# Inverse and decays of a delta rule, and two scalings of a state space, moved to GpSimd in a planned layer kernel

## The chip, the cores and the metric

The kernel runs on one core of a Trainium2 chip. The metric is device time in microseconds (us), the median of several executions; smaller is better. The engines are TensorE (PE in the rows, its weight loads PEld), VectorE (DVE), ScalarE (ACT), GpSimd (POOL) and the DMA queue of SyncE (SP).

## The reference

One layer of a hybrid mixer in float32: 1024 tokens and 256 context tokens, model width 2048. After a modulated RMS norm and one wide projection `u @ w_in`, half of the width goes through a state space (16 heads of 64, state 128) and half through a gated delta rule (8 heads of 128), both in both directions and in chunks of 128 tokens; then gating, norms, the output projection and a residual. What the change touches:

```python
# delta rule, per head, direction and chunk
decay = exp(where(incl, gcum[..., :, None] - gcum[..., None, :], -inf))
a_strict = where(strict, einsum('bhcik,bhcjk->bhcij', k_beta, k) * decay, 0.0)
sol = triangular_solve(a_strict, rhs, lower=True, unit_diagonal=True)
attn = einsum('bhcik,bhcjk->bhcij', q, k) * decay
# state space, per group and direction
lmat = exp(where(causal, seg, -inf))                      # seg: difference of cumulated decays
y_diag = einsum('bcgrqs,bcsgrp->bcqgrp', cb * lmat, xdt)  # xdt = x * dt
states = einsum('bcsgn,bcsgrp->bcgrpn', bm, xdt * decay_end)
```

## The kernel before, in words

The projection runs in blocks of 128 output channels. A block's weights come as two raw tiles, are split into a high and a low half in float16 (`split`: squares and first half on ScalarE, L410 and L413, second half on VectorE, L415), and three products per block of 128 inputs are summed on TensorE (`products`, L439), 512 tokens at a time into PSUM banks `ps_d` and `ps_e`. `conv_block` empties a bank: one ScalarE instruction (L492, L494), four VectorE instructions for the other taps (L500), a tanh (L504) and a product (L505). The taps are scaled by one small GpSimd instruction per block (L485).

The eight heads of the delta rule follow one another as a pipeline, written in `steps` of `build` and listed as: `P` (`gdn_prep` of head h+1), `C` (`gdn_chain` of head h), the projection blocks of head h+2 with `E` (`gdn_end` of h) between them, `V` (`gdn_post` of h+2), a gate block `z`, `I` (`invert` of head h+1).

- `gdn_prep` takes ten chunks. Per chunk a DMA broadcasts a row of cumulated decays to `gb` (four buffers), `decay` (L678) makes min(gb - G, mask) on VectorE for each of the two directions, ScalarE takes the exponential, TensorE forms the products of keys, and VectorE makes the matrix `A`.
- `invert_blocks` then writes the diagonal 32x32 blocks of `A` to DRAM, loads them as `X` (80 rows, each a block), and inverts all of them by 30 steps of two dependent VectorE instructions (L728 and L730, of (31-k)*k elements in step k). `X` goes back by DMA and comes in as `xc`, which `invert` turns into the whole inverses with small TensorE products. `X` shares its buffer with the keys of `gdn_post`.
- `gdn_chain` is the recurrence: ten steps in each direction, each a sequence of TensorE products and VectorE or ScalarE instructions (`r`, `xw`, `S`). Once both directions of a pair of chunks are done, `finish_pair` scales them: a square on ScalarE (L831) and five small instructions on GpSimd (L833, L834, a power at L129, L836, L837). `gdn_end` transposes the result on TensorE (L98 into `ps_c`).

Then come four quarters of the state space (`ssd_quarter`), again with projection blocks between them. `state` scales x by `dtw` in four ScalarE instructions (L943) per chunk and direction; the decays `E` of a chunk come by DMA and get their biases in eight ScalarE instructions (L991). GpSimd does the decay of the state (L951) and adds the two directions (L1001). The output projection (L1140) ends the kernel.

All engines' orders are written out ahead by the class `Plan`: it simulates the program with a table of costs per instruction and, from 450 us of its own time on, lets each engine take the ready instruction of the lowest priority number. The number is the place in the program, lowered by a million for instructions that write the tiles in `FIRST`. Its gap between dependent instructions of one engine is zero:

```python
    FIRST = ("ps_c0", "ps_c1", "r0", "r1", "xw0", "xw1", "S0", "S1", "o", "ps_h", "ps_z", "xd", "H0", "H1", "y0", "y1")
...
            gap = 0 if max(k, q) >= real or (e == self.engine[q] and not self.dma[k]) else self.AFTER.get(e, 90)
```

On the chip each engine then runs its own list in that order, and waits at its head.

Of the kernel before, what the change touches and what calls it, by code (L numbers as in the profile page):

```python
# [13 lines left out]
AF = mybir.ActivationFunctionType  # L14
ALU = mybir.AluOpType

P = 128
# [6 lines left out]
NCH = T // P  # L24
# [22 lines left out]
class Layer:  # L47
# [627 lines left out]
    def decay(self, e, d, h, c):  # L675

        nc = self.nc
        nc.vector.scalar_tensor_tensor(out=e, in0=e, scalar=self.G[:, 32 + d * 8 + h, c:c + 1],  # L678
                                       in1=self.mneg[:, d], op0=ALU.subtract, op1=ALU.min)

    def gdn_prep(self, h, D):
        nc, sp = self.nc, self.gp
# [3 lines left out]
        for c in range(NCH):  # L686
            gb = t_([P, 2, P], "gb", bufs=GB)
            nc.sync.dma_start(out=gb, in_=self.gr[32:48, c * P:(c + 1) * P].rearrange("(d h) t -> h d t", d=2)[h]
                              .partition_broadcast(P))
            for d in range(2):  # L690
                self.decay(gb[:, d], d, h, c)
# [6 lines left out]
            for d in range(2):  # L698
                nc.vector.scalar_tensor_tensor(out=A[:, d, c], in0=gb[:, d], scalar=D["nb"][:, d, c:c + 1],
                                               in1=pk[:, 0:P], op0=ALU.mult, op1=ALU.mult)  # L700
# [6 lines left out]
    def invert_blocks(self, A):  # L707

        nc, sp = self.nc, self.gp
        t_ = lambda shape, name, **kw: sp.tile(shape, F32, tag=name, name=name, **kw)  # L710
        Q = 2 * NCH
# [9 lines left out]
        X = t_([P, NCH * P], "X")[0:4 * Q, 0:1024].rearrange("p (a b) -> p a b", b=32)  # L721
        tp = t_([4 * Q, 256], "tp")
        nc.sync.dma_start(out=X, in_=d1.rearrange("q b j i -> (q b) j i"))
        for k in range(1, 31):
            m = 31 - k
            t = tp[:, 0:m * k].rearrange("p (a b) -> p a b", b=k)
            sh = [4 * Q, m, k]
            nc.vector.tensor_tensor(out=t, in0=X[:, k + 1:, k:k + 1].to_broadcast(sh),  # L728
                                    in1=X[:, k:k + 1, 0:k].to_broadcast(sh), op=ALU.mult)
            nc.vector.tensor_tensor(out=X[:, k + 1:, 0:k], in0=X[:, k + 1:, 0:k], in1=t, op=ALU.add)  # L730
# [186 lines left out]
    def ssd_quarter(self, Q, xT, BT, CT):  # L917
        nc, sp = self.nc, self.sp
        t_ = lambda shape, name, **kw: sp.tile(shape, F32, tag=name, name=name, **kw)
        R, PD = 4, 64  # L920
        hs = [slice(d * 16 + Q * R, d * 16 + Q * R + R) for d in range(2)]
        bc = lambda ap, n: ap.unsqueeze(2).to_broadcast([P, R, n])
# [17 lines left out]
        def state(d, c, H, first):  # L940
            xd = t_([P, R, PD], "xd", bufs=3)
            for r in range(R):
                nc.scalar.activation(out=xd[:, r], in_=xs[:, c, r], func=AF.Copy, scale=self.dtw[:, hs[d].start + r, c:c + 1])  # L943
# [37 lines left out]
        for i, c in enumerate([8, 9, 0, 1, 2, 3, 4, 5, 6, 7]):  # L981
            s = slice(c * P, (c + 1) * P)
            if c < NLC:
# [4 lines left out]
                for d in range(2):  # L988
                    for r in range(R):
                        j = d * 16 + Q * R + r  # L990
                        nc.scalar.activation(out=E[:, d, r], in_=E[:, d, r], func=AF.Identity, bias=self.G[:, j, c:c + 1])  # L991
# [303 lines left out]
class Plan:  # L1295
# [5 lines left out]
    ACT = ((1, 190), (64, 335), (128, 362), (256, 413), (512, 600), (1024, 1070))  # L1301
# [45 lines left out]
    def time(self, k, i, outs, ins):  # L1347
# [19 lines left out]
        return table(self.POOL) if n != NCH else 900  # L1367
# [155 lines left out]
```

## Time and profile before

| | us |
|---|---|
| median of three runs | 2345.31 |
| lowest and highest | 2343.54, 2347.75 |
| the profiled execution | 2343.03 |
| its span, first to last instruction | 2341.3 |
| TensorE busy in it | 2143.4 |
| VectorE busy | 1439.1 |
| ScalarE busy | 1004.1 |
| GpSimd busy | 270.2 |
| mean granted TensorE clock | 0.964 |

The profile is of one execution. Busy time leaves out waits. The granted clock is a share of full speed: 1.0 is 2.4 GHz and 0.5 is 1.2 GHz. A wait is put down to whatever came last before the waiting instruction began.

### The profile page before, as it was taken

How to read it: one execution, taken by the hardware profiler on the slowest of the kernel's cores; microseconds unless marked ns; L12 is line 12 of the kernel's file. 1: busy time of each engine (PE TensorE's matmuls, PEld its weight loads, DVE VectorE, ACT ScalarE, POOL GpSimd, SP SyncE). 2: the span in 40 equal slices, each digit the busy share in tenths (PEclk: the TensorE clock that was granted, in tenths of full speed). 3: DMA queues.
4: the chain of work that ended last, by engine and by line, in shares of the span. 5: the costliest groups of instructions: out<-in, count | busy, mean ns of one | idle time of the engine just before them, and what ended most of it. 6: DMA issues, size and time to landing. Idle time of an engine off the chain costs nothing.

```text
span 2341.3 us, 41797 instructions
## 1 busy us (share of the span) xinstructions
PE 2143.4 (92%) x16070; PEld 1402.3 (60%) x16070; DVE 1439.1 (61%) x3499; ACT 1004.1 (43%) x2493; POOL 270.2 (12%) x514
## 2 busy tenths in 40 slices
PE   4989998989889989899898999999999998899997
PEld 4334644456564656547565566755646565788886
DVE  5335542778885785858859578667777763511214
ACT  6026421443435253353533434475767574423320
POOL 1000000011112020210302101130303030000000
PEclk9999999999999999999899999999999999899999
DMA  9952246444443434444444453334365445112117
GB/s 321 348 169 56 80 151 189 110 123 117 131 116 109 124 104 120 105 117 116 123 105 99 113 136 110 90 110 121 107 199 142 125 134 207 55 37 73 55 38 269
DMA packets 397236, 301.71 MB, mean 129 GB/s; under 512 B 61339, under 2 KB 358684, under 8 KB 395628
## 3 DMA queue, kind: packets, MB, share of 16 engines
q1 hardware_dynamic: 386668, 293.80, 43.5%
q10 hardware_dynamic: 10368, 5.24, 0.8%
q8 instruction: 126, 2.06, 0.4%
q14 instruction: 74, 0.61, 0.1%
HBM read 241.41 MB, written 57.57 MB: 128 GB/s over the span
## 4 chain that ended last, share of the span: by engine, by line
PE 68%; DVE 14%; DMA 11%; issue 3%; ACT 3%; SPq 1%; POOL 1%; DVEq 0%; ACTq 0%; POOLq 0%
PE ps_d L439 28%; PE ps_d L1140 12%; PE ps_e L439 9%; DVE cv L500 3%; DMA gb<-gr 3%; DVE X L730 2%; DVE tp L728 2%; PE ps_m L327 2%; DMA u<-in_w_out_dram 1%; PE ps_d L253 1%; DMA X<-d 1%; PE ps_m L253 1%; DMA d<-ft 1%; PE ps_m L439 1%; PE ps_c L878 1%
## 5 line engine op out<-in xcount | busy, mean ns | idle before, releaser
L439 PE MATMUL ps_d<-u,w 128*128 128x512 f16 (+1 forms) x4560 | 963.8, 356 | 23.2 <-DVE cv L500 16.8
L439 PEld LDWEIGHTS <-w 128*128 128x128 f16 x6048 | 596.2, 100 | 527.1 <-issue 57.7
L1140 PEld LDWEIGHTS <-u 128*128 128x128 f16 x3072 | 301.6, 99 | 56.3 <-DMA u<-in_w_out_dram 12.0
L439 PE MATMUL ps_e<-u,w 128*128 128x512 f16 (+1 forms) x1296 | 314.3, 379 | 13.0 <-ACT w L413 8.6
L500 DVE SCALAR_TENSOR_TENSOR cv<-ps_d,taps,cv 128x496 f32<-128x496 f32 (+3 forms) x300 | 195.4, 654 | 68.1 <-ACT cv L492 44.1
L1140 PE MATMUL ps_d<-wx,u 128*128 128x256 f16 x1536 | 170.2, 273 | 3.8 <-DMA u<-in_w_out_dram 3.8
L410 ACT ACTIVATE w<-w 128x1024 f16<-128x1024 f32 (+1 forms) x102 | 106.2, 1042 | 134.7 <-DMA w<-in_w_in_dram 92.0
L415 DVE SCALAR_TENSOR_TENSOR w<-w,scl 128x512 f16<-128x512 f32 (+1 forms) x204 | 146.6, 756 | 27.7 <-ACT w L413 27.1
L1140 PE MATMUL ps_d<-w,u 128*128 128x256 f16 x1296 | 146.6, 274 | 6.0 <-DMA u<-in_w_out_dram 3.4
L1170 DVE SCALAR_TENSOR_TENSOR raw<-ps_d,inv,gp 128x256 f32<-128x256 f32 x59 | 28.4, 482 | 191.1 <-ACT jko L1168 191.1
L413 ACT ACTIVATE w<-w,scl 128x1024 f16<-128x1024 f32 (+1 forms) x102 | 112.8, 1132 | 32.2 <-DVE inv L162 19.0
L1168 ACT ACTIVATE jko<-ps_d,inv 128x256 f32<-128x256 f32 x59 | 27.8, 472 | 184.1 <-PE ps_d L1140 179.4
L875 ACT ACTIVATE r<-ps_c,nb 128x128 f32<-128x128 f32 x128 | 46.5, 365 | 130.3 <-DVE xw L873 117.5
L504 ACT ACTIVATE t<-cv 128x512 f32<-128x512 f32 (+1 forms) x98 | 55.7, 570 | 86.9 <-DVE cv L500 70.7
L991 ACT ACTIVATE E<-E,G 128x128 f32<-128x128 f32 x256 | 81.0, 388 | 24.6 <-DMA E<-gr 23.2
L728 DVE TENSOR_TENSOR tp<-X 80x30 f32<-80x30 f32 (+14 forms) x240 | 80.8, 337 | 15.9 <-DMA X<-d 10.2
L730 DVE TENSOR_TENSOR X<-X,tp 80x30 f32<-80x30 f32 (+14 forms) x240 | 79.3, 330 | 6.2
L943 ACT ACTIVATE xd<-xs,dtw 128x64 f32<-128x64 f32 x288 | 76.1, 336 | 15.7 <-PE ps_h L945 14.4
L500 DVE SCALAR_TENSOR_TENSOR cv<-ps_e,taps,cv 128x496 f32<-128x496 f32 (+3 forms) x92 | 65.6, 713 | 13.9 <-ACT cv L492 12.2
L678 DVE SCALAR_TENSOR_TENSOR gb<-gb,G,mneg 128x128 f32<-128x128 f32 x160 | 50.8, 357 | 36.3 <-DMA gb<-gr 29.3
L505 DVE SCALAR_TENSOR_TENSOR cv<-t,cv 128x512 f32<-128x512 f32 (+1 forms) x98 | 60.7, 620 | 16.2 <-ACT t L504 15.8
L485 POOL TENSOR_SCALAR taps<-cw_gdn,inv 128x5 f32<-128x5 f32 x24 | 8.6, 358 | 520.3 <-DVE inv L162 497.8
(329 smaller groups left out, 3262.7 us busy)
## 6 DMA issues: line engine op xcount, KB each, us to landing
w<-in_w_in_dram SPq DMA_DIRECT2D x102, 512.0 KB, 4.8
x<-in_w_ada_dram SPq DMA_DIRECT2D x48, 1024.0 KB, 9.3
vq<-vq SPq DMA_DIRECT2D x128, 256.0 KB, 2.8
E<-gr SPq DMA_DIRECT2D x64, 256.0 KB, 4.9
u<-in_w_out_dram SPq DMA_DIRECT2D x24, 512.0 KB, 3.6
gb<-gr SPq DMA_DIRECT2D x80, 128.0 KB, 4.6
x<-in_x_dram SPq DMA_DIRECT2D x8, 1024.0 KB, 4.9
vq<-gb SPq DMA_DIRECT2D x64, 128.0 KB, 3.3
```

What stands on the lines that cost most here:

```text
L410: nc.scalar.activation(out=w16[h][:, 0], in_=w[h], func=AF.Square, accum_out=ssq[:, h:h + 1])
L413: nc.scalar.activation(out=w16[h][:, 0], in_=w[h], func=AF.Copy, scale=t)
L415: nc.vector.scalar_tensor_tensor(out=w16[h][:, 1, s], in0=w[h][:, s], scalar=t, in1=w16[h][:, 0, s], op0=ALU.mult, op1=ALU.subtract)
L439: self.nc.tensor.matmul(out=ps, lhsT=w16[k // KH][:, a, k % KH], rhs=self.u16[b][k][:, lo:lo + n], start=(k == 0 and i == 0), stop=(k == K ...
L500: nc.vector.scalar_tensor_tensor(out=o3[:, :, lo_o:hi_o], in0=p3[:, :, lo_o + s:hi_o + s], scalar=taps[tap], in1=o3[:, :, lo_o:hi_o], op0= ...
L504: nc.scalar.activation(out=t[:, 0:n], in_=o, func=AF.Tanh)
L505: nc.vector.scalar_tensor_tensor(out=o, in0=t[:, 0:n], scalar=1.0, in1=o, op0=ALU.add, op1=ALU.mult)
L728: nc.vector.tensor_tensor(out=t, in0=X[:, k + 1:, k:k + 1].to_broadcast(sh), in1=X[:, k:k + 1, 0:k].to_broadcast(sh), op=ALU.mult)
L730: nc.vector.tensor_tensor(out=X[:, k + 1:, 0:k], in0=X[:, k + 1:, 0:k], in1=t, op=ALU.add)
L943: nc.scalar.activation(out=xd[:, r], in_=xs[:, c, r], func=AF.Copy, scale=self.dtw[:, hs[d].start + r, c:c + 1])
L991: nc.scalar.activation(out=E[:, d, r], in_=E[:, d, r], func=AF.Identity, bias=self.G[:, j, c:c + 1])
L1140: self.nc.tensor.matmul(out=ps, lhsT=self.y16(k, p, s), rhs=w16[k // 4][:, q, k % 4], start=(i == 0 and j == 0), stop=(i == KB - 1 and j = ...
```

## The change

The 60 instructions of the inverse per head go from VectorE to GpSimd. The decay of a chunk, two VectorE instructions of subtract and min with the mask, becomes three GpSimd instructions: subtract and min with 0 per direction, and one addition of the mask over both. The x scaling of `state`, four ScalarE instructions, becomes one on GpSimd with a broadcast factor, and the eight biases of a chunk's `E` become two on GpSimd. In the plan's cost tables the largest ScalarE entries rise (512 elements from 600 to 640 ns, 1024 from 1070 to 1110), a GpSimd power costs 400 + 155 ns per element instead of the table's value, and a GpSimd instruction of the tensor-scalar kind 290 + 3.45 ns per element; the table for the other GpSimd instructions stays.

```diff
-    def decay(self, e, d, h, c):
+    def decay(self, e, h, c):
         nc = self.nc
-        nc.vector.scalar_tensor_tensor(out=e, in0=e, scalar=self.G[:, 32 + d * 8 + h, c:c + 1],
-                                       in1=self.mneg[:, d], op0=ALU.subtract, op1=ALU.min)
+        for d in range(2):
+            nc.gpsimd.tensor_scalar(out=e[:, d], in0=e[:, d], scalar1=self.G[:, 32 + d * 8 + h, c:c + 1], scalar2=0.0,
+                                    op0=ALU.subtract, op1=ALU.min)
+        nc.gpsimd.tensor_tensor(out=e, in0=e, in1=self.mneg, op=ALU.add)
...
-            for d in range(2):
-                self.decay(gb[:, d], d, h, c)
+            self.decay(gb, h, c)
...
-            nc.vector.tensor_tensor(out=t, in0=X[:, k + 1:, k:k + 1].to_broadcast(sh),
+            nc.gpsimd.tensor_tensor(out=t, in0=X[:, k + 1:, k:k + 1].to_broadcast(sh),
                                     in1=X[:, k:k + 1, 0:k].to_broadcast(sh), op=ALU.mult)
-            nc.vector.tensor_tensor(out=X[:, k + 1:, 0:k], in0=X[:, k + 1:, 0:k], in1=t, op=ALU.add)
+            nc.gpsimd.tensor_tensor(out=X[:, k + 1:, 0:k], in0=X[:, k + 1:, 0:k], in1=t, op=ALU.add)
...
-            for r in range(R):
-                nc.scalar.activation(out=xd[:, r], in_=xs[:, c, r], func=AF.Copy, scale=self.dtw[:, hs[d].start + r, c:c + 1])
+            nc.gpsimd.tensor_tensor(out=xd, in0=xs[:, c], in1=bc(self.dtw[:, hs[d], c], PD), op=ALU.mult)
...
-                    for r in range(R):
-                        j = d * 16 + Q * R + r
-                        nc.scalar.activation(out=E[:, d, r], in_=E[:, d, r], func=AF.Identity, bias=self.G[:, j, c:c + 1])
+                    nc.gpsimd.tensor_tensor(out=E[:, d], in0=E[:, d], in1=bc(self.G[:, hs[d], c], P), op=ALU.add)
...
-    ACT = ((1, 190), (64, 335), (128, 362), (256, 413), (512, 600), (1024, 1070))
+    ACT = ((1, 190), (64, 335), (128, 362), (256, 413), (512, 640), (1024, 1110))
     POOL = ((1, 250), (128, 520), (256, 736), (512, 1194))
...
-        return table(self.POOL) if n != NCH else 900
+        if getattr(i, "op", None) == ALU.pow:
+            return 400 + 155 * n
+        return 290 + 3.45 * n if kind == "InstTensorScalarPtr" else table(self.POOL)
```

## Rows read from the trace of the kernel before

**Rows 1.** The page, part 1: busy time of each engine, share of the span, instructions.

```profile
PE 2143.4 (92%) x16070; PEld 1402.3 (60%) x16070; DVE 1439.1 (61%) x3499; ACT 1004.1 (43%) x2493; POOL 270.2 (12%) x514
```

**Rows 2.** Busy time by stage: the delta rule's and the state space's. The columns are the stage, its length, busy time of each engine with the number of instructions, granted clock, DMA share and GB/s.

```profile
...
410.00:1520.00 1110.00, 1028.84 (x7966) 658.82 (x7965) 830.76 (x2259) 452.15 (x1174) 159.94 (x315) 0.96 0.43 114
1520.00:1960.00 440.00, 415.20 (x2411) 248.28 (x2410) 306.54 (x644) 301.82 (x814) 87.00 (x148) 0.98 0.51 147
...
```

**Rows 3.** TensorE's waits in the delta rule's stage (410 to 1520 us): who waited for whom, us in total, times, the longest.

```profile
PE ps_c L98 <- POOL o L837: 21.2, 6, 4.7
PE ps_d L439 <- DVE cv L500: 11.6, 3, 10.6
PE ps_e L439 <- ACT w L413: 8.6, 1, 8.6
```

**Rows 4.** The seven stretches in that stage in which TensorE stands still the longest, one per head, columns as in rows 2.

```profile
473.50:482.20 8.70, 0.06 (x2) 0.04 (x2) 7.88 (x28) 1.82 (x3) 0.47 (x2) 0.72 0.18 45
...
1270.70:1277.60 6.90, 0.60 (x5) 0.36 (x4) 6.45 (x20) 0.74 (x4) 4.07 (x7) 0.65 0.36 91
sum 50.00, PE 3.87 PEld 2.38 DVE 46.40 ACT 5.29 POOL 19.84; mean PE 0.55 PEld 0.34 DVE 6.63 ACT 0.76 POOL 2.83
```

**Rows 5.** The stretches of the low clock beside them, from the point where TensorE has work again in the first two, whole in the other five, columns as in rows 2.

```profile
482.20:487.60 5.40, 5.40 (x14) 2.03 (x15) 3.73 (x8) 3.00 (x5) 0.00 (x0) 0.50 1.05 214
...
sum 63.50, PE 38.28 PEld 19.01 DVE 59.23 ACT 26.28 POOL 23.29; mean PE 5.47 PEld 2.72 DVE 8.46 ACT 3.75 POOL 3.33
```

**Rows 6.** Two heads' inverses, one after the other, from the first instruction to the last, columns as in rows 2.

```profile
958.10:987.50 29.40, 24.28 (x169) 18.22 (x167) 27.42 (x95) 6.89 (x26) 8.20 (x19) 0.97 0.21 62
1101.10:1130.50 29.40, 24.45 (x165) 18.26 (x163) 27.42 (x95) 6.88 (x26) 8.20 (x19) 0.92 0.21 59
...
```

**Rows 7.** Groups of the page, part 5, that the change removes: line, engine, operation, tiles, shapes, count, then busy time, mean ns of one, and idle time before them with what ended it.

```profile
L991 ACT ACTIVATE E<-E,G 128x128 f32<-128x128 f32 x256 | 81.0, 388 | 24.6 <-DMA E<-gr 23.2
L728 DVE TENSOR_TENSOR tp<-X 80x30 f32<-80x30 f32 (+14 forms) x240 | 80.8, 337 | 15.9 <-DMA X<-d 10.2
L730 DVE TENSOR_TENSOR X<-X,tp 80x30 f32<-80x30 f32 (+14 forms) x240 | 79.3, 330 | 6.2
L943 ACT ACTIVATE xd<-xs,dtw 128x64 f32<-128x64 f32 x288 | 76.1, 336 | 15.7 <-PE ps_h L945 14.4
L678 DVE SCALAR_TENSOR_TENSOR gb<-gb,G,mneg 128x128 f32<-128x128 f32 x160 | 50.8, 357 | 36.3 <-DMA gb<-gr 29.3
```

**Rows 8.** The end of one inverse as a timeline, of VectorE, GpSimd and TensorE in turn: start, us, instruction, count, and in brackets the idle time before it and what ended it.

```profile
1130.32 0.19 DVE L730 TENSOR_TENSOR X<-X,tp 80x30 f32<-80x30 f32 x1
1130.43 2.06 DVE L415 SCALAR_TENSOR_TENSOR w<-w,scl 128x512 f16<-128x512 f32 x3
1132.41 3.05 DVE L500 SCALAR_TENSOR_TENSOR cv<-ps_d,taps,cv 128x496 f32<-128x496 f32 x4
...
1130.51 2.04 POOL L836 TENSOR_TENSOR ss<-ss,si 128x2 f32<-128x2 f32 x1
1132.63 0.62 POOL L837 TENSOR_TENSOR o<-o,ss 128x256 f32<-128x256 f32 x1
...
1133.30 0.48 PE L98 MATMUL ps_c<-ident,o 128*128 128x128 f32 x1 [4.39 <-POOL o L837]
```

**Rows 9.** Single lines on GpSimd: count, shortest/median/longest duration in ns, first and last start, shape.

```profile
L837 POOL TENSOR_TENSOR o<-o,ss x32: 614/720/1084, 555.7 to 1517.9; 128x256 f32<-128x256 f32 x32
L836 POOL TENSOR_TENSOR ss<-ss,si x32: 197/258/2046, 555.5 to 1517.6; 128x2 f32<-128x2 f32 x32
L1001 POOL TENSOR_TENSOR cv<-y,cv x64: 447/457/993, 1561.4 to 1921.3; 128x128 f32<-128x128 f32 x64
L666 POOL TENSOR_TENSOR cv<-cv,kn x24: 616/1040/1488, 407.9 to 1305.7; 128x512 f32<-128x512 f32 x16, 128x256 f32<-128x256 f32 x8
L485 POOL TENSOR_SCALAR taps<-cw_gdn,inv x24: 306/322/799, 240.1 to 1240.7; 128x5 f32<-128x5 f32 x24
L129 POOL TENSOR_TENSOR ss<-ss,mhalf x32: 705/714/847, 554.7 to 1516.8; 128x2 f32<-128x2 f32 x32
```

**Rows 10.** Groups on GpSimd with every shape kept apart, columns as in rows 7.

```profile
L951 POOL TENSOR_TENSOR H<-H,cd 128x256 f32<-128x256 f32 x64 | 45.4, 709 | 108.6 <-DVE H L952 61.3 <-ACT H L949 46.2 <-PE ps_z L964 0.3
L837 POOL TENSOR_TENSOR o<-o,ss 128x256 f32<-128x256 f32 x32 | 22.6, 706 | 2.5
```

**Rows 11.** One head's `xc` after the inverse: VectorE's first use, and TensorE's.

```profile
998.90 0.84 DVE L743 STREAM_TRANSPOSE xt<-xc 128x640 f32<-128x640 f32 x1
...
L766 PE MATMUL ps_m<-xc,A x40: 191/191/212, 1038.7 to 1039.4; 32*32 32x32 f32 x40
```

**Rows 12.** The decays of one head's last seven chunks (14 instructions), columns as in rows 9.

```profile
L678 DVE SCALAR_TENSOR_TENSOR gb<-gb,G,mneg x14: 343/346/352, 1065.5 to 1097.2; 128x128 f32<-128x128 f32 x14
```

**Rows 13.** Waits in the state space's stage (1520 to 1960 us), of TensorE and of ScalarE, columns as in rows 3.

```profile
PE ps_y L1005 <- DVE E L998: 3.6, 6, 1.2
PE ps_d L439 <- ACT E L993: 3.5, 1, 3.5
...
ACT E L991 <- DMA E<-gr: 23.2, 21, 4.6
```

**Rows 14.** VectorE's splits of the weights in the delta rule's stage, columns as in rows 7.

```profile
L415 DVE SCALAR_TENSOR_TENSOR w<-w,scl 128x512 f16<-128x512 f32 x128 | 92.2, 761 | 19.8 <-ACT w L413 19.2
```

## The prediction, made before the changed kernel was run

> **What bounds the kernel now.** I read the busy times first [rows 1]: TensorE is busy for 92% of the span, so no saving elsewhere can bring more than TensorE's idle time and what its low clock costs. The table by stage says where these are [rows 2]. In the delta rule's stage TensorE is busy for 1028.8 of 1110 us, 81 us idle, and VectorE for 831 us. In the state space's stage TensorE is idle for 25 of 440 us, with VectorE and ScalarE each busy for about 300. GpSimd is nearly free in both (160 and 87 us).
>
> Third, TensorE's waits in the delta rule's stage [rows 3]: three kinds lead, for the last scaled output of a chain (L837 on GpSimd), for VectorE to empty a bank (L500), and for ScalarE's weights. Looking for them in time gives seven stretches, one per head, 50.0 us with 3.9 us of TensorE work in them, so 46.1 us idle [rows 4]. VectorE is busy for 46.4 of the 50 us: it is the engine to look at. Around each stretch the granted clock is 0.50, that is 1.2 instead of 2.4 GHz, for about 10 us, after the idle time has begun. In these stretches TensorE does 38.3 us of work [rows 5]; at the full level half of that would do, so 19.1 us are lost. Together a head loses (46.1 + 19.1) / 7 = 9.3 us.
>
> Fourth, what VectorE does there. From the first instruction of an inverse to its last 29.4 us pass, 27.4 of them busy [rows 6]. The inverse's 60 instructions are (80.8 + 79.3) / 8 = 20.0 us of a head [rows 7]. Their place in the program is ahead of the chain and of the next blocks, and the plan takes the lowest number first; only the chain's `FIRST` tiles pass them. What that leaves is in the timeline [rows 8]: 0.11 us after the start of the inverse's last instruction VectorE begins three weight splits, then four instructions to empty a bank, one after the other without a pause. These had waited for it, and TensorE for them. In the same timeline the GpSimd multiply of a 128x2 tile (L836) takes 2.04 us, beside the three splits of together 2.06 us; its shortest run is 0.197 us [rows 9]. TensorE's transposes wait for it.
>
> **The change, part by part.** *Inverse.* It removes 20.0 us of VectorE per head and puts 60 dependent instructions of 9920 elements in all ((31-k)*k, summed twice over k) on GpSimd. Undisturbed, 2 elements take 0.197 us and 128 elements with two full inputs 0.447 [rows 9], so 0.193 us and 1.98 ns per element; between dependent ones lie 2.5/32 = 0.08 us [rows 10]. That is 60 * 0.271 + 9920 * 0.00198 = 35.9 us. From below, half of the elements at the broadcast rate (0.614 us for 256 elements [rows 9], 1.64 ns each) give 34.2. From above I take the dearest rate in the case, the diff's own 3.45 ns: 50.4 us. I take 35.9, since the nearest rows give it. The old inverse took 29.4 us from end to end, so `xc` comes 6.5 us later, at worst 21. TensorE first uses `xc` 40 us after VectorE could [rows 11], and in between it has blocks to multiply; so this costs nothing. Without that cover it would be 7 * 6.5 = 46 us. Next late is `gdn_post`, which needs the buffer of `X`; its results are due a whole period later, 143 us [rows 6].
>
> *Decays.* VectorE loses 2 * 0.357 us per chunk and 57 us in all, and with them its waits for the `gb` DMA, 36.3 us [rows 7]; these now hold GpSimd's queue. A chunk costs GpSimd one 256-element addition (0.193 + 256 * 0.00198 = 0.70 us) and two subtractions with a per-row scalar. No row has these at 128 elements. From below the 0.31 us of 5 elements [rows 9], from above the diff's 290 + 3.45 * 128 = 732 ns. I take the upper one: its formula gives 307 ns at 5 elements, where the trace has 306 to 322 [rows 9]. So 2.2 us and three gaps of 0.08, 2.4 us per chunk (1.6 at the low end), 24 us per head, 1.7 us longer than before for each chunk. Seven chunks take 32 us [rows 12], some 5 us each, which is twice what GpSimd needs, so the delay is paid once: hidden, like the inverse's, by the 40 us before `xc` is used.
>
> GpSimd's load in a head becomes 160/8 + 36 + 24 = 80 of 143 us. What stands behind the inverse in its queue are the four `finish_pair` groups (about 2.4 us each) of the other head's chain: the inverse's number is lower and its next instruction always ready, so the plan lets it pass. `gdn_end` waits for them, with its transposes (L98) in TensorE's list. The plan knows it, as far as its prices hold. Its table gives the inverse 34.6 us, against my 35.9: 1.3 us late. One burst of splits as above [rows 8] adds 2.04 - 0.20 = 1.8 us. So TensorE meets a transpose 3.1 us too early, 7 * 3.1 = 22 us. The corrected power helps: 710 ns for two elements, where the trace has 714 [rows 9] and the old table 252; part of the 21.2 us of L98's waits [rows 3] came from this.
>
> The Trainium skill (SBUF — State Buffer, Who interferes with whom) speaks against the change: a VectorE instruction with two SBUF inputs and a GpSimd instruction that reads SBUF share one read interface, and whichever starts first holds it for its whole duration. The trace agrees, with the 2.04 us of L836. By that rule alone, with no free interface, the sum is that of the fourth case below; by the rows of one burst it is the term above.
>
> *State space.* 76.1 + 81.0 = 157 us of ScalarE go [rows 7]. GpSimd gets 72 multiplies of 256 elements (0.614 to 0.709 us [rows 9, 10], 47 us) and 64 additions of 512 (1.04 us [rows 9], 67 us): 201 of 440 us. The latency falls too, from four times 0.336 to 0.66 us for `xd` and from eight times 0.388 to 2.1 us for a chunk's biases. Waits for the `E` DMA, 23.2 us on ScalarE [rows 13], now hold the state's products on GpSimd instead. TensorE's waits that hang on these results are 7.1 us [rows 13]; I take half, 3.5 us, from nothing to 25 (all its idle time there). If GpSimd's queue holds `xd` behind a late DMA, as much could be lost.
>
> *Plan.* The new prices reorder every engine's list from 450 us on. I have no row for that; 10 us either way.
>
> The sum: 46.1 + 19.1 - 22 + 3.5 = 46.7 us. The profiled execution took 2343.0 us (span 2341.3), 2.3 below the median of 2345.3. So 2343.0 - 46.7 + 2.3 = 2298.6; I say 2299.
>
> **The rivals.** *More* (chance 0.23): GpSimd is not late, all 65 us come back, and the shorter chain takes some of the other 35 us of idle time in the stage (81 - 46) and of the 25 in the state space. 65 + 20 to 35 is 2245 to 2260. For it: VectorE falls from 27.4 to 17 of 29.4 us there, about half its load. Against it: short waits of a recurrence stay, whoever is busy.
>
> *Nothing* (0.07): the wait for VectorE turns into one of the same length for GpSimd, and the plan's change moves little. 2341 to 2350. For it: already now TensorE waits for L837 six times [rows 3].
>
> *Slower* (0.18): the read interface. All splits of a head, 92.2/8 = 11.5 us [rows 14], fall into the inverse and hold it. It takes 47.4 us, 12.8 more than planned; each head's transposes stand at TensorE's head for as long, and the low clock follows as now (19.1/7 = 2.7 us). That is 15.5 us lost for 9.3 gained, 7 * 6.2 = 43 us: 2389. It decides once GpSimd is more than 9.3 - 2.7 = 6.6 us late per head. An inverse at the dear rate, 50 us, would do the same. For it: L836's 2.04 us, and that half of the inverse reads two full inputs. Against it: splits are two bursts of a few us per block, spread over the period, and VectorE waits as well when GpSimd holds the interface.
>
> **How the numbers follow.** The forecast has 0.52, from 2275 to 2330 by its terms: late by nothing (22 us more) at the low end, by twice the 3.1 us (22 less) with a bad order (10) at the high end. The range reaches from 2250, which leaves out half of *more*'s lower part (0.05), to 2355, which leaves out most of *slower* (0.13). What a measurement can tell from no change is 0.2%, 4.7 us: faster 0.52 + 0.23 = 0.75, same 0.07, slower 0.18.
>
> **What would show it.** Right: no stretch of over 3 us without TensorE work at a head's inverse, no low clock there, splits and L500 that begin while GpSimd inverts, TensorE idle for some 45 us in the delta rule's stage instead of 81, an inverse of 34 to 42 us on GpSimd. Wrong: TensorE's L98 waits for L837 with more than 21 us in total, an inverse near 50 us, a 128-element subtraction far from 0.73 us, `xc` that TensorE waits for, or idle time of ScalarE that TensorE gets nothing from while `ps_h` waits for `xd`.

## The result: 31.5 us faster, two thirds of the forecast

The changed kernel takes 2315.03 us (median of 4 runs, 2309.04 to 2316.66), the kernel before beside it 2346.53 us (4 runs): a ratio of 0.9853, 95% interval 0.9825 to 0.9881. That is 31.5 us less where the sum gave 46.7, inside the range. The profiled executions are 2315.8 and 2343.0 us, with spans of 2314.1 and 2341.3, so the traces hold 27.2 of the 31.5 us. One execution, of the run *prices 15% higher still* below, took 3205 us at a granted clock of 0.65 and is left out of its ratio.

Line numbers after: the decays are L679 and L681, the inverse L729 and L731, the finishing of a chain's output L834 to L838 (L833 to L837 before), `xd` L943, the biases of `E` L989.

From the page of the kernel after, busy times, which answer [rows 1]:

```profile
PE 2137.2 (92%) x16070; PEld 1400.6 (61%) x16070; DVE 1293.1 (56%) x2859; ACT 852.7 (37%) x1949; POOL 824.2 (36%) x1370
```

TensorE's share has not moved. VectorE and ScalarE lost about 150 us each, and GpSimd gained 554. The chain that ended last (the page of after, share by engine) now has GpSimd in second place; its inverse is 12 of the 15%:

```profile
PE 57%; POOL 15%; DMA 10%; DVE 9%; issue 4%; ACT 3%; SPq 1%; DVEq 0%; POOLq 0%; ACTq 0%
```

To see which stage the time came from I cut both traces at the same events instead of the same times: first decay, first copy of `xs`, first weight load of the output projection.

| stage | before: us, TensorE idle | after: us, TensorE idle | change |
|---|---|---|---|
| start | 402.8, 62.0 | 407.3, 63.3 | +4.5 |
| delta rule | 1130.1, 82.3 | 1094.8, 57.6 | -35.3 |
| state space | 425.8, 22.8 | 429.8, 25.4 | +4.0 |
| output | 382.6, 30.8 | 382.2, 30.5 | -0.4 |

The start has the same code in both; over all the kernels here it took 402.7 to 409.8 us. The gain is all in the delta rule's stage. These windows give it, before and then after, with the columns of [rows 2]:

```profile
402.80:1532.90 1130.10, 1047.80 (x8065) 669.08 (x8064) 838.19 (x2275) 461.67 (x1196) 164.11 (x321) 0.96 0.43 114
```
```profile
407.30:1502.10 1094.80, 1037.21 (x8060) 668.52 (x8058) 666.53 (x1635) 456.39 (x1196) 590.36 (x1042) 0.98 0.44 117
```

TensorE does the same work in 10.6 us less, and is idle 24.7 us less: together the 35.3. The mean clock rises from 0.96 to 0.98, but that is not where most of the 10.6 us come from: of the 31 us that the low clock lasts less, TensorE was idle for 28 (the sums are in the part on why the prediction was right or wrong). For whom it waits there (410 to 1500 us of after, which answers [rows 3]):

```profile
PE ps_c L98 <- POOL o L838: 31.6, 8, 6.6
PE ps_c L879 <- ACT r L876: 7.5, 8, 2.0
PE ps_e L439 <- DVE cv L500: 4.8, 2, 2.6
```

The waits for VectorE's L500 are small now. Those for GpSimd's finished output have grown from 21.2 to 31.6 us. In time they are one stretch in each of six heads. Windows of the first and the last of six, with their sum, which answer [rows 4]:

```profile
616.50:622.50 6.00, 0.01 (x1) 0.00 (x0) 1.67 (x2) 0.78 (x1) 5.12 (x15) 0.81 0.19 55
...
1254.20:1258.10 3.90, 0.01 (x1) 0.00 (x0) 2.58 (x4) 0.63 (x1) 3.33 (x11) 1.00 0.41 102
sum 30.00, PE 0.03 PEld 0.02 DVE 6.80 ACT 2.04 POOL 25.18; mean PE 0.01 PEld 0.00 DVE 1.13 ACT 0.34 POOL 4.20
```

In [rows 4] VectorE was busy for 46.4 of 50 us; here it is busy for 6.8 of 30, and GpSimd for 25.2. Behind each stretch the clock is low again, as in [rows 5], though for less: 27.45 us of TensorE's work in 37.5 us, where the seven of before had 38.28 in 63.5. The last of the six windows, and their sum:

```profile
1258.50:1261.90 3.40, 3.40 (x9) 1.21 (x8) 0.00 (x0) 0.00 (x0) 2.88 (x8) 0.50 1.04 203
sum 37.50, PE 27.45 PEld 11.56 DVE 2.40 ACT 11.72 POOL 31.83; mean PE 4.58 PEld 1.93 DVE 0.40 ACT 1.95 POOL 5.31
```

One such stretch as a timeline (after; start, us, instruction):

```profile
1119.18 0.25 POOL L731 TENSOR_TENSOR X<-X,tp 80x30 f32<-80x30 f32 x1
1119.37 0.15 POOL L732 MEMSET X<- 80x32 f32 x1
1119.45 0.19 POOL L834 TENSOR_TENSOR ss<-ss,s 128x2 f32<-128x2 f32 x1
...
1120.05 0.73 POOL L129 TENSOR_TENSOR ss<-ss,mhalf 128x2 f32<-128x2 f32 x1
...
1121.14 0.62 POOL L838 TENSOR_TENSOR o<-o,ss 128x256 f32<-128x256 f32 x1
1121.81 0.38 PE L98 MATMUL ps_c<-ident,o 128*128 128x128 f32 x1 [4.32 <-POOL o L838]
1121.98 2.34 PE L439 MATMUL ps_e<-u,w 128*128 128x512 f16 x5
```

The last multiply-add of the inverse ends, the first finishing group runs right behind it, and TensorE, whose list has the transposes here, has stood for 4.32 us. Matmuls that need nothing of it come behind. The inverse itself (windows of two heads of after, which answer [rows 6]) is 37 us long with 32 us of GpSimd's work:

```profile
946.80:983.90 37.10, 32.86 (x209) 22.17 (x207) 21.95 (x53) 14.00 (x37) 32.48 (x61) 0.97 0.30 86
1082.60:1119.40 36.80, 33.86 (x213) 22.75 (x211) 25.61 (x61) 13.18 (x37) 32.15 (x61) 1.00 0.31 83
```

The moved groups on the page of after, which answer [rows 7], and two that were not moved:

```profile
L729 POOL TENSOR_TENSOR tp<-X 80x30 f32<-80x30 f32 (+14 forms) x240 | 126.0, 525 | 33.2 <-DMA X<-d 15.0
L731 POOL TENSOR_TENSOR X<-X,tp 80x30 f32<-80x30 f32 (+14 forms) x240 | 135.1, 563 | 18.8
L679 POOL TENSOR_SCALAR gb<-gb,G 128x128 f32<-128x128 f32 x160 | 120.8, 766 | 205.0 <-DMA gb<-gr 88.2
L943 POOL TENSOR_TENSOR xd<-xs,dtw 128x256 f32<-128x256 f32 x72 | 52.2, 729 | 73.6 <-ACT xs L939 56.6
L989 POOL TENSOR_TENSOR E<-E,G 128x512 f32<-128x512 f32 x64 | 74.7, 1172 | 63.9 <-DMA E<-gr 63.6
L415 DVE SCALAR_TENSOR_TENSOR w<-w,scl 128x512 f16<-128x512 f32 (+1 forms) x204 | 165.4, 845 | 35.5 <-ACT w L413 34.8
L500 DVE SCALAR_TENSOR_TENSOR cv<-ps_d,taps,cv 128x496 f32<-128x496 f32 (+3 forms) x300 | 195.4, 653 | 74.8 <-ACT cv L492 41.2
```

### The profile page after: what moved, and what is told of

Its sections match the earlier page's. It is cut to its first block, busy times and chain, and to the rows that moved or that the text cites. A ratio compares the mean times of both kernels' runs of the same rounds, so it can differ in the third digit from the quotient of the medians.

```text
span 2314.1 us, 41521 instructions
## 1 busy us (share of the span) xinstructions
PE 2137.2 (92%) x16070; PEld 1400.6 (61%) x16070; DVE 1293.1 (56%) x2859; ACT 852.7 (37%) x1949; POOL 824.2 (36%) x1370
## 4 chain that ended last, share of the span: by engine, by line
PE 57%; POOL 15%; DMA 10%; DVE 9%; issue 4%; ACT 3%; SPq 1%; DVEq 0%; POOLq 0%; ACTq 0%
PE ps_d L439 20%; PE ps_d L1138 12%; POOL X L731 6%; PE ps_e L439 6%; POOL tp L729 6%; DMA gb<-gr 3%; PE ps_m L327 2%; PE ps_d L253 1%; PE ps_m L98 1%; DMA u<-in_w_out_dram 1%; PE ps_m L253 1%; DVE w L415 1%; DVE cv L500 1%; DMA X<-d 1%; POOL gb L679 1%
## 5 line engine op out<-in xcount | busy, mean ns | idle before, releaser
L439 PE MATMUL ps_d<-u,w 128*128 128x512 f16 (+1 forms) x4560 | 974.4, 356 | 4.4 <-ACT w L413 2.8
L500 DVE SCALAR_TENSOR_TENSOR cv<-ps_d,taps,cv 128x496 f32<-128x496 f32 (+3 forms) x300 | 195.4, 653 | 74.8 <-ACT cv L492 41.2
L679 POOL TENSOR_SCALAR gb<-gb,G 128x128 f32<-128x128 f32 x160 | 120.8, 766 | 205.0 <-DMA gb<-gr 88.2
L415 DVE SCALAR_TENSOR_TENSOR w<-w,scl 128x512 f16<-128x512 f32 (+1 forms) x204 | 165.4, 845 | 35.5 <-ACT w L413 34.8
L731 POOL TENSOR_TENSOR X<-X,tp 80x30 f32<-80x30 f32 (+14 forms) x240 | 135.1, 563 | 18.8
L729 POOL TENSOR_TENSOR tp<-X 80x30 f32<-80x30 f32 (+14 forms) x240 | 126.0, 525 | 33.2 <-DMA X<-d 15.0
L1168 DVE SCALAR_TENSOR_TENSOR raw<-ps_d,inv,gp 128x256 f32<-128x256 f32 x59 | 28.3, 482 | 191.6 <-ACT jko L1166 191.6
L413 ACT ACTIVATE w<-w,scl 128x1024 f16<-128x1024 f32 (+1 forms) x102 | 113.2, 1134 | 50.7 <-DVE scl L147 27.6
L989 POOL TENSOR_TENSOR E<-E,G 128x512 f32<-128x512 f32 x64 | 74.7, 1172 | 63.9 <-DMA E<-gr 63.6
L500 DVE SCALAR_TENSOR_TENSOR cv<-ps_e,taps,cv 128x496 f32<-128x496 f32 (+3 forms) x92 | 65.5, 712 | 50.4 <-ACT cv L492 42.0
L505 DVE SCALAR_TENSOR_TENSOR cv<-t,cv 128x512 f32<-128x512 f32 (+1 forms) x98 | 67.2, 687 | 21.9 <-ACT t L504 21.3
L943 POOL TENSOR_TENSOR xd<-xs,dtw 128x256 f32<-128x256 f32 x72 | 52.2, 729 | 73.6 <-ACT xs L939 56.6
```

What stands on the lines that cost most here:

```text
L413: nc.scalar.activation(out=w16[h][:, 0], in_=w[h], func=AF.Copy, scale=t)
L415: nc.vector.scalar_tensor_tensor(out=w16[h][:, 1, s], in0=w[h][:, s], scalar=t, in1=w16[h][:, 0, s], op0=ALU.mult, op1=ALU.subtract)
L439: self.nc.tensor.matmul(out=ps, lhsT=w16[k // KH][:, a, k % KH], rhs=self.u16[b][k][:, lo:lo + n], start=(k == 0 and i == 0), stop=(k == K ...
L500: nc.vector.scalar_tensor_tensor(out=o3[:, :, lo_o:hi_o], in0=p3[:, :, lo_o + s:hi_o + s], scalar=taps[tap], in1=o3[:, :, lo_o:hi_o], op0= ...
L505: nc.vector.scalar_tensor_tensor(out=o, in0=t[:, 0:n], scalar=1.0, in1=o, op0=ALU.add, op1=ALU.mult)
L679: nc.gpsimd.tensor_scalar(out=e[:, d], in0=e[:, d], scalar1=self.G[:, 32 + d * 8 + h, c:c + 1], scalar2=0.0, op0=ALU.subtract, op1=ALU.min)
```

## The experiments

Two questions: which part of the change brings the gain, and what keeps the rest from coming. The expectations name theories by letters. A is that the gain is VectorE's relief from the inverse; B, that it is the corrected prices; C, that the other moves bring something too, not the inverse alone. D is that the waits at L98 come from GpSimd's queue order, the finishing groups behind the inverse. E is that a delay taken away in one place comes back in another. F is that the waits come from the plan's prices: GpSimd is later than the plan thinks. G and H are F's rivals: the prices hardly matter, and a gain by new prices is only a lucky order.

All were timed beside the kernel before on the same chip (2347.9 to 2349.0 us there); the ratios go by that neighbour. The stages are cut as above, the waits are TensorE's L98 for the finished output, 410 to 1500 us.

| kernel | median us | ratio, 95% | delta rule | state space | waits |
|---|---|---|---|---|---|
| before (first runs) | 2346.5 | | 1130.1 | 425.8 | 21.2 |
| after | 2315.0 | 0.9853 (0.9825 to 0.9881) | 1094.8 | 429.8 | 31.6 |
| prices alone | 2357.3 | 1.0041 (1.0025 to 1.0057) | 1127.4 | 435.1 | 16.3 |
| prices, inverse | 2315.5 | 0.9854 (0.9838 to 0.9871) | 1086.4 | 438.1 | 28.5 |
| after, scalings back | 2318.3 | 0.9877 (0.9856 to 0.9898) | 1088.9 | 438.8 | 32.9 |
| after, inverse back | 2332.6 | 0.9933 (0.9918 to 0.9947) | 1115.5 | 425.7 | 12.8 |
| after, old prices | 2313.8 | 0.9859 (0.9843 to 0.9875) | 1097.0 | 426.4 | 29.0 |
| after, finish first | 2313.6 | 0.9841 (0.9822 to 0.986) | 1092.5 | 426.7 | 28.3 |
| after, measured prices | 2295.1 | 0.9781 (0.9761 to 0.9801) | 1076.1 | 429.6 | 16.8 |
| measured prices, finish first | 2316.6 | 0.9865 (0.9848 to 0.9882) | 1093.6 | 430.1 | 13.0 |
| after, decays back | 2301.5 | 0.9801 (0.9783 to 0.9818) | 1081.7 | 428.3 | 27.2 |
| prices 15% higher still | 2301.1 | 0.9797 (0.978 to 0.9815) | 1076.6 | 431.2 | 8.0 |
| inverse alone, measured prices | 2297.0 | 0.9776 (0.9755 to 0.9797) | 1065.8 | 443.3 | 8.9 |
| after, another order | 2307.2 | 0.9822 (0.9803 to 0.9842) | 1086.4 | 428.2 | 28.3 |

### Which part brings the gain

**Prices alone.** The kernel before with the diff's new table, nothing moved.

```diff
-    ACT = ((1, 190), (64, 335), (128, 362), (256, 413), (512, 600), (1024, 1070))
+    ACT = ((1, 190), (64, 335), (128, 362), (256, 413), (512, 640), (1024, 1110))
-            return table(self.POOL) if n != NCH else 900
+        if getattr(i, "op", None) == ALU.pow:
+            return 400 + 155 * n
+        return 290 + 3.45 * n if kind == "InstTensorScalarPtr" else table(self.POOL)
```

> The kernel before with the new cost tables alone; all instructions stay on their engines. Theory A (the gain is VectorE's relief from the inverse): the inverse still holds VectorE ahead of the splits and of L500, so TensorE's stretches without work stay at 4 to 10 us per head, and the time is 2333 to 2350 us; of TensorE's 21.2 us of waits for L837 some go, as the power is priced right. Rival B (the gain is the corrected plan): 2305 to 2322 us, like the changed kernel.

Measured: 8.3 us slower than before. The delta rule's stage stays (1127.4), the state space loses 9 us. TensorE's waits show the old kind still there (410 to 1500 us):

```profile
PE ps_c L98 <- POOL o L837: 16.3, 6, 3.2
PE ps_e L439 <- DVE cv L500: 14.3, 4, 9.9
PE ps_m L98 <- ACT X L644: 12.2, 4, 3.1
```

So the new prices bring nothing by themselves, and B fell; the time lies 7 us above A's range.

**Prices and the inverse.** The same with L728 and L730 on GpSimd.

```diff
-            nc.vector.tensor_tensor(out=t, in0=X[:, k + 1:, k:k + 1].to_broadcast(sh),
+            nc.gpsimd.tensor_tensor(out=t, in0=X[:, k + 1:, k:k + 1].to_broadcast(sh),
-            nc.vector.tensor_tensor(out=X[:, k + 1:, 0:k], in0=X[:, k + 1:, 0:k], in1=t, op=ALU.add)
+            nc.gpsimd.tensor_tensor(out=X[:, k + 1:, 0:k], in0=X[:, k + 1:, 0:k], in1=t, op=ALU.add)
```

> The kernel before with the new cost tables and only the inverse on GpSimd; decays stay on VectorE, scalings and biases of the state space on ScalarE. Theory A: most of the gain is here, 2305 to 2325 us, and TensorE still waits for the last scaled output (L837 in before) with 20 to 35 us, since the inverse goes first on GpSimd. Rival C (it takes all four moves, decays and ScalarE's relief too): 2330 to 2345 us.

Measured: 2315.5, the time of the whole change, as A has it. That is 33.5 us less than before, and 41.8 less than the prices alone, 41.0 of them in the delta rule's stage. The wait for GpSimd is there too:

```profile
PE ps_c L98 <- POOL o L837: 28.5, 8, 5.8
```

**The scalings back on ScalarE** (`xd` and the biases of `E` as before, all else as after).

```diff
-            nc.gpsimd.tensor_tensor(out=xd, in0=xs[:, c], in1=bc(self.dtw[:, hs[d], c], PD), op=ALU.mult)
+            for r in range(R):
+                nc.scalar.activation(out=xd[:, r], ..., scale=self.dtw[:, hs[d].start + r, c:c + 1])
-                    nc.gpsimd.tensor_tensor(out=E[:, d], in0=E[:, d], in1=bc(self.G[:, hs[d], c], P), op=ALU.add)
+                    for r in range(R):
+                        j = d * 16 + Q * R + r
+                        nc.scalar.activation(out=E[:, d, r], ..., bias=self.G[:, j, c:c + 1])
```

> The changed kernel with the scaling of x and the biases of E back on ScalarE. Theory A: ScalarE was not what TensorE waited for in the state space, so within 6 us of the changed kernel's 2315, on either side. Rival C: 157 us more on ScalarE bring TensorE's waits back, 2325 to 2340 us.

Measured: 3.3 us slower than after, with overlapping intervals; A held and C fell. By stage the state space loses 9.0 us and the delta rule, where these lines do not run, gains 5.9 by another order.

**The inverse back on VectorE** (the second diff reversed, in the kernel after).

> The changed kernel with the inverse back on VectorE; decays, scalings and biases stay on GpSimd, the plan's prices stay. Theory A (the inverse alone is the gain): 2338 to 2355 us, with TensorE's stretches without work at the end of each inverse as before. Rival C (decays and ScalarE's relief carry a part): 2320 to 2335 us.

Measured: 2332.6 (0.9933), in C's range, so without the inverse the change is worth 15 us against before, and 25 against the prices alone (0.9933 / 1.0041 = 0.9892). By stage, against the prices alone: 11.9 us in the delta rule, where only the decays differ, and 9.4 in the state space, where only the scalings do. These parts do not add to the inverse's 41.8: moved last, after the others, the inverse brings 17.6 us (2332.6 to 2315.0). With the inverse on GpSimd the decays' 11.9 are not seen again, and the state space comes out where it was before any change. The waits (410 to 1500 us) are spread over the recurrence:

```profile
PE ps_c L853 <- DVE o L892: 13.2, 9, 3.8
PE ps_c L98 <- POOL o L838: 12.8, 4, 3.7
PE ps_e L439 <- DVE w L415: 5.5, 1, 5.5
```

**Decays back on VectorE** (L678 as before, all else as after).

```diff
-        for d in range(2):
-            nc.gpsimd.tensor_scalar(out=e[:, d], in0=e[:, d], scalar1=..., scalar2=0.0, op0=ALU.subtract, op1=ALU.min)
-        nc.gpsimd.tensor_tensor(out=e, in0=e, in1=self.mneg, op=ALU.add)
+        nc.vector.scalar_tensor_tensor(out=e, in0=e, scalar=..., in1=self.mneg[:, d], op0=ALU.subtract, op1=ALU.min)
```

> The changed kernel with the decays back on VectorE (57 us there, and its waits for their DMA). Theory A (VectorE has room once the inverse is gone): within 8 us of the changed kernel's 2315. Rival C (the decays carry a part of their own, as they seem to when the inverse stays on VectorE, where e6 is 15 us under the kernel before): 2323 to 2332 us.

Measured: 2301.5, 13.6 us less than after (12.2 by the ratios), and 13.1 less in the delta rule's stage. Neither expectation held. The waits at L98 are 27.2 us, 4.4 less than after, so most of the gain is elsewhere.

### What keeps the rest from coming

**Old prices** (the kernel after, with the table of before; the first diff reversed).

> The changed kernel with the old cost tables. Theory F (TensorE meets the transposes as much too early as the plan prices GpSimd's queue too low): a power at 252 instead of 710 ns adds 1.8 us over four pairs and a subtraction at 520 instead of 766 ns more, so the waits for L838 grow from 31.6 to 40 us or more, and the time to 2318 to 2335 us. Rival G (the prices hardly matter): within 5 us of 2315.

Measured: 2313.8, no difference from after, as G has it. The waits did not grow to 40 us but are 29.0: here F's forecast fell. What the diff corrects (the power, the subtraction, ScalarE's largest) is not what matters; the inverse's price, 34.6 us, is the same in both tables. The state space is 426.4 us, as before the change.

**Finish first.** The tile `ss` of the finishing groups joins `FIRST`, so they pass the inverse in the plan.

```diff
-    FIRST = (..., "xd", "H0", "H1", "y0", "y1")
+    FIRST = (..., "xd", "H0", "H1", "y0", "y1", "ss")
```

> The changed kernel with the tile ss added to the plan's FIRST, so that the four scalings of a finished pair of chunks go on GpSimd between the instructions of the inverse, not behind it. Theory D (what is left of the loss is the queue on GpSimd: TensorE waits 31.6 us for L838, with the low clock after it): these waits fall under 8 us, the inverse ends up to 10 us later, which is hidden, and the time is 2275 to 2297 us. Rival E (GpSimd is late by its own load or by the read interface shared with VectorE, so that the delay only moves to the keys of the next head or to xc): the waits for L838 go, others of the same size come, 2306 to 2320 us.

Measured: 2313.6, no difference. The groups did pass: their last instruction starts 5 to 36 us after the start of an inverse instead of 38 to 47 us, and the inverse stretches from some 37 us to between 45 and 47. TensorE waits all the same (timeline, same head as above):

```profile
1117.30 0.62 POOL L731 TENSOR_TENSOR X<-X,tp 80x228 f32<-80x228 f32 x1
1117.88 0.20 POOL L834 TENSOR_TENSOR ss<-ss,s 128x2 f32<-128x2 f32 x1
...
1119.55 0.62 POOL L838 TENSOR_TENSOR o<-o,ss 128x256 f32<-128x256 f32 x1
1120.22 0.48 PE L98 MATMUL ps_c<-ident,o 128*128 128x128 f32 x1 [5.37 <-POOL o L838]
1120.77 0.65 POOL L731 TENSOR_TENSOR X<-X,tp 80x220 f32<-80x220 f32 x1
```

The group stands between two instructions of the inverse now, and TensorE's list has the transposes earlier too: here 32 us after the start of the inverse, where they stood 39 us after it. So D fell: TensorE waits as long (28.3 us in all) with the groups in another place of the queue. E's time range held, but not its sign, that these waits go. That the work ahead of the group takes longer than the plan has it, wherever the group stands, would explain this; the next runs try it.

**Measured prices.** The kernel after; the plan's prices of GpSimd are set to what its trace shows, with the pause between dependent instructions in them. The inverse then has about 38 us in the plan instead of 34.6.

```diff
-    POOL = ((1, 250), (128, 520), (256, 736), (512, 1194))
+    POOL = ((1, 285), (30, 357), (128, 545), (240, 790), (256, 835), (512, 1260))
-            return 400 + 155 * n
-        return 290 + 3.45 * n if kind == "InstTensorScalarPtr" else table(self.POOL)
+            return 480 + 155 * n
+        return 360 + 3.85 * n if kind == "InstTensorScalarPtr" else table(self.POOL)
```

> The changed kernel with GpSimd priced in the plan as its trace has it, with the 0.08 us between dependent instructions: 357 ns at 30 elements, 545 at 128, 790 at 240, 835 at 256, 1260 at 512, so 37.8 us for an inverse (34.6 in the table before, 37.1 measured); a power 480 + 155 ns per element, a subtraction 360 + 3.85. Theory F: TensorE's waits for L838 fall from 31.6 to under 12 us, the low clock with them, and the time is 2280 to 2300 us. Rival E (the delay moves to another wait of the same size): 2308 to 2320 us.

Measured: 2295.1, 20 us less than after (17 by the ratios), 18.7 of them in the delta rule's stage: there TensorE is idle 49.3 us instead of 57.6, and busy 10.4 us less. The time is as F has it. The wait is halved, but not under 12 us, and 6.5 of the 14.8 us that it lost came back in other waits:

```profile
PE ps_c L98 <- POOL o L838: 16.8, 8, 7.4
```

**Measured prices and finish first.** Both edits together.

> As e8, and the tile ss in the plan's FIRST as in e4, so that the scalings of a finished pair pass the inverse. Theory F: with true prices the order is free to matter; the transposes come early and without a wait, 2275 to 2300 us. Rival E: 2308 to 2320 us.

Measured: 2316.6. The named waits fall further, to 13.0 us, but the gain is gone, as E has it: with finish first, the measured prices are worth nothing (2313.6 and 2316.6). Another wait takes their place (TensorE, 410 to 1500 us):

```profile
PE ps_m L98 <- ACT X L644: 15.7, 5, 12.1
```

Its longest case in the timeline:

```profile
628.06 0.15 POOL L732 MEMSET X<- 80x32 f32 x1
...
628.24 0.34 SPq L733 DMA_DIRECT2D d<-X  x1
...
630.92 0.59 ACT L644 COPY X<-ps_m 128x512 f32<-128x512 f32 x1
...
631.56 0.69 PE L98 MATMUL ps_m<-ident,cv 128*128 128x128 f32 x2 [12.07 <-ACT X L644]
```

The inverse, stretched to 44 to 47 us by the groups within it, keeps the buffer `X` until its DMA has read it. The next head's keys are copied into that buffer, and TensorE's transposes stand behind the copy for 12 us.

**Prices 15% higher still** (the inverse has 43.6 us in the plan).

```diff
-    POOL = ((1, 285), (30, 357), (128, 545), (240, 790), (256, 835), (512, 1260))
+    POOL = ((1, 300), (30, 410), (128, 630), (240, 910), (256, 960), (512, 1450))
```

> As e8, with GpSimd's elementwise prices another 15% up (an inverse 43.6 us in the plan, 37 on the chip). Theory F (TensorE waits as much as the plan prices GpSimd's queue too low): the waits for L838 fall from e8's 16.8 to under 6 us and the time stays within 8 us of e8's 2295, as the transposes now come late at no cost. Rival H (e8's gain over the changed kernel is a lucky order, no mechanism): waits and time fall back to 25 us and more, and 2308 to 2322 us.

Measured: 2301.1, within 8 us of the run with measured prices, as F has it, and not back at 2308, as H has it. The wait is down to 8.0 us in two cases (F: under 6), and others come up (410 to 1500 us):

```profile
PE ps_e L439 <- DVE cv L500: 9.9, 2, 7.7
PE ps_c L98 <- POOL o L838: 8.0, 2, 7.6
PE ps_y L98 <- ACT btok L930: 7.3, 1, 7.3
```

**The inverse alone, measured prices** (the kernel "prices, inverse" with the prices of "after, measured prices").

> As e2 (only the inverse on GpSimd), with the prices of e8. Theory F: the waits for the last scaled output fall from 28.5 us to under 15 and the time from 2315 to 2290 to 2303 us, without the other three moves. Rival H: 2308 to 2322 us.

Measured: 2297.0, 18.5 us less than with the diff's prices, 20.6 less in the delta rule's stage, where TensorE is idle 37.2 us instead of 51.3. F held in both numbers. The wait is short in every case:

```profile
PE ps_c L98 <- POOL o L837: 8.9, 11, 2.4
```

**Another order.** The kernel after with the plan's `lead` at 520 instead of 500 ns, which means nothing to the work.

```diff
-    nc = build(Plan(*build(None), lead=500, fixed=450e3))[0]
+    nc = build(Plan(*build(None), lead=520, fixed=450e3))[0]
```

> The changed kernel with the plan's lead before TensorE at 520 instead of 500 ns: another order of every engine with no reason behind it, as a measure of what a new order alone can do. Theory F: 2308 to 2322 us, the waits for L838 between 24 and 38 us. Rival H: as far from 2315 as e8 is, 20 us on either side.

Measured: 2307.2, just below F's range and 8 us less than after, with nearly the same waits at L98 (28.3). So this reorder alone moves the time by some 8 us for no reason of its own. It is one reorder; how far others go was not tried. What is not clearly larger than that here can't be put down to the edit. Two pairs with measured prices (18.5 and 20 us) are above it, and both times the wait that F names falls by about half or more: 31.6 to 16.8, 28.5 to 8.9. In the third pair, with finish first, that wait falls too (28.3 to 13.0), but another takes its place and nothing is gained. Lower prices for GpSimd's power and subtraction alone ("old prices") did not make the wait longer. So that an inverse priced below what it takes makes TensorE wait here is well supported; that F is the whole gain of the two pairs is not shown.

## Why the prediction was right or wrong

**What bounds the kernel: right.** The idle stretch at each head came from VectorE, and what takes the inverse off VectorE takes the stretch away: 41.8 us by the inverse alone against the prices alone, 33.5 against before. No other part is needed for the change's time.

**Seven stretches, less a new wait: right in the sum, by luck.** The prediction had 46.1 - 22 = 24.1 us less idle time in the delta rule's stage, and measured are 24.7 (82.3 to 57.6). Two misses cancel. The new waits are 31.6 us and not 22; the idle time outside the stretches fell by 8.6, from 36.2 to 27.6 us (82.3 - 46.1, 57.6 - 30.0), which the forecast had left to the case *more*.

**The low clock: wrong, and this is the step that failed most.** I took back all of the 19.1 us and kept 22 us of new waits. The case *slower* says itself that the low clock follows a wait; the sum did not. These are the sums over all stretches of the low clock in the stage, eight before and then ten after (their length, then each engine's busy time in them, in sum and on average):

```profile
sum 81.93, PE 43.74 PEld 22.09 DVE 72.94 ACT 32.67 POOL 26.70; mean PE 5.47 PEld 2.76 DVE 9.12 ACT 4.08 POOL 3.34
```
```profile
sum 51.20, PE 41.03 PEld 19.19 DVE 11.46 ACT 19.36 POOL 38.64; mean PE 4.10 PEld 1.92 DVE 1.15 ACT 1.94 POOL 3.86
```

TensorE did 43.7 us of its work at the low level before, and does 41.0 us after: 27.4 behind the six new stretches and 13.6 in four other places. At the full level half would do, so the low clock cost 21.9 us and still costs 20.5: 1.4 us came back of the 19.1.

**What made up for it: not forecast.** TensorE's busy time fell by 10.6 us, so 9.2 us of it lie at the full level. The prediction had that nothing but idle time and low clock can be saved; the cause of these 9.2 us is open. Term by term, the traces' 27.2 us are 24.7 less idle (forecast 24.1), 1.4 of the clock (19.1), -4.0 in the state space (3.5), and outside the forecast 9.2 at the full level, -4.5 in the start and 0.4 in the output. So that the time came as near as it did is in part luck, and the range, 2250 to 2355 us, would have held the time of before as well.

**GpSimd's lateness: the mechanism right, its size short.** The four finishing groups stand behind the inverse, and TensorE meets its transposes too early: 31.6 / 7 = 4.5 us per head and not 3.1. The inverse itself came as said: 36.8 to 38.3 us in six heads, 37.4 on average, where the prediction had 35.9 and 1.8 for one burst of splits, 37.7 together. In the trace the inverse's instructions beside a split take 2.1 us per head more than the usual time of their size. The plan has 34.6, so 2.8 us of the 4.5 would be the plan's price, which fits that measured prices take about half of the waits away or more. What the other 1.7 us are is open.

**The decays: wrong.** The delay was to be "hidden, like the inverse's"; put back on VectorE they make the kernel 13.6 us faster. Their durations were as predicted (0.766 us for 0.732, 0.746 for 0.70). With the inverse on VectorE they are worth 11.9 us of the stage; that this is VectorE's relief is likely, not shown. With the inverse gone no run shows a gain from moving them. How much it costs is open. "Scalings back" against "prices, inverse" differ by the decays too, and there they cost 2.9 us of the time (2318.3 to 2315.5), within what an order does. "Another order" alone gives 8 of the 13.6, so the cost may lie anywhere from nothing to 14 us.

**The state space: wrong by 7.5 us.** +4.0 and not -3.5. `xd` and the biases cost what was said or a little more (0.729 us, 1.172 for 1.04). In the same plan the move to GpSimd is worth 9 to 14 us of that stage (438.8 to 429.8; 438.1 to 428.3; 443.3 to 429.6). But the new prices, with the work on ScalarE, had cost 9 to 12 against before (435.1 and 438.1 for 425.8). With the old prices and the work on GpSimd it is 426.4. So 145 us of ScalarE's time were worth nothing there, against before.

**The signs.** The inverse's length and the price of the subtraction came as said. Six stretches of 3.9 to 6.6 us at the inverse, the low clock behind them and 31.6 us at L98 (sign of wrong: more than 21) went against it. The prediction is not at one with itself there: its sum keeps 22 us of these waits, and leaves 81 - 46.1 + 22 = 57 us idle, while its sign of right has 45. Measured are 57.6.

**The rivals.** *More* did not come: GpSimd was late. *Nothing* neither. *Slower*: its mechanism is in the trace. From the kernel with measured prices and finish first:

```profile
620.48 0.47 POOL L729 TENSOR_TENSOR tp<-X 80x168 f32<-80x168 f32 x1
621.03 0.53 POOL L731 TENSOR_TENSOR X<-X,tp 80x168 f32<-80x168 f32 x1
...
621.40 3.30 DVE L415 SCALAR_TENSOR_TENSOR w<-w,scl 128x512 f16<-128x512 f32 x4 [0.99 <-ACT w L413]
621.64 0.82 POOL L729 TENSOR_TENSOR tp<-X 80x150 f32<-80x150 f32 x1
...
622.53 0.80 POOL L731 TENSOR_TENSOR X<-X,tp 80x150 f32<-80x150 f32 x1
...
625.08 0.37 POOL L729 TENSOR_TENSOR tp<-X 80x108 f32<-80x108 f32 x1
```

Beside a burst of splits an instruction of the inverse takes 0.8 us, where a larger one just before took 0.5 (the kernel after shows the same). The Trainium skill (SBUF — State Buffer, Who interferes with whom) has it so, for VectorE instructions with two SBUF inputs. The trace agrees: L415's mean on the page rose from 756 to 845 ns, while L500, with one input from PSUM, stayed at 654 and 653. Run by run, in the trace of after, the 82 splits of 512 elements with no GpSimd instruction beside them took 745 ns on average and at most 753, the 118 with one 927. But the burst ends after a few us, as the counter-argument had it: the inverse was 37.4 us, not 47.4. What this sharing costs the whole kernel no run separated.

**What the change leaves.** Several runs beat both kernels. The two fastest are the change with measured prices (2295.1, 0.9781) and the inverse alone with them (2297.0, 0.9776), which do not differ by what a run here can tell. The second has the shortest delta rule (1065.8) and the longest state space (443.3); the inverse and the scalings on GpSimd, decays on VectorE, measured prices, might join the good stages of both, and was not tried.

## What to carry to other kernels

Move what the loaded engine has to get rid of, and ask of each further piece whether it still relieves anybody once the first has gone: here the inverse alone brought the time of the whole change, and with it gone 180 us of decays on the new engine showed no gain. Where lists are fixed ahead by prices, give the new engine its measured ones, with the pause between dependent instructions: in two of three pairs measured prices were worth another 17 to 20 us, in the third another wait took the gain. One new order without a reason moved the time by 8 us, so a single faster run is no proof of its reason. And when a sum keeps a wait, let it keep what follows the wait too, here the low clock.

## What the runs showed of the hardware

- One full input instead of two was not cheaper on GpSimd here: the subtraction and min of 128 elements with a per-row scalar (L679) takes 0.708 us at its shortest and 0.716 in the middle, where an addition of two full 128-element inputs takes 0.447 at its shortest [rows 9].
- Low clock followed short idle stretches of TensorE: the granted clock is 1.00 in the last stretch shown above, of 3.9 us, and 0.50 (1.2 instead of 2.4 GHz) for 3.4 us behind it. The longest, of 6.6 us, is followed by 5.9 us of work at 0.50, and a wait of 2.0 us (to 1323.0 us, after) by 3.4 us at 0.50.
- VectorE's L415 (two SBUF inputs) and GpSimd slow each other: L415 takes 745 ns alone and 927 beside a GpSimd instruction, 1.60 us at the longest, and beside it the inverse's instructions of 150 elements take 0.8 us where 0.44 to 0.49 is usual. L500 (one PSUM input) takes 740 ns at 504 elements alone and 738 beside one.
